# RMSNorm and QKV projection on one core: a longer hand-laid order, and row tiles moved between TensorE and the DMA crossbar

## The chip, the cores and the metric

One core of a Trainium2 chip runs the kernel. Its engines work side by side, each through its own queue of instructions in order: TensorE (PE in the profile, PEld for its weight loads) multiplies matrices and writes PSUM; VectorE (DVE), ScalarE (ACT) and GpSimd (POOL) do elementwise work; SyncE (SP) issues the DMAs, which sixteen DMA engines carry out. The metric is the device time of one execution in microseconds (us), the median of several runs.

## The reference

```python
def reference(x, gamma, w_qkv, eps):
    rms = np.sqrt(np.mean(x ** 2, axis=-1, keepdims=True) + eps)
    x_norm = x / rms * gamma
    return np.matmul(x_norm, w_qkv).astype(np.float32)
```

`x` is 8 x 1024 rows of 768 numbers, `w_qkv` is 768 x 2304, all float32; `gamma` has 768 entries. So 8192 rows are normalised and multiplied into 8192 x 2304 outputs.

## The kernel before

**Tiles.** The 8192 rows are 64 row tiles of 128. A matrix product on TensorE contracts over partitions, so each row tile has to be transposed: its 768 columns become six blocks of 128 x 128 (`xT`). The weights come in 16 pieces (`load_w`), are multiplied by gamma and turned to bf16 (`conv`) into `w_b`.

**Two methods.** Row tiles 0 to 3 are multiplied plainly (`mm`, six blocks per 512 columns), and their results scaled and copied out (`evac`, `store`). All other tiles go in pairs, pair p being tiles 2p and 2p+1, by Strassen-Winograd's seven products in place of eight. For this the 2304 columns are three chunks c of 768, and both operands are cut into quarters: tile 2p gives a11 and a12, tile 2p+1 gives a21 and a22; the weights of a chunk give b11 to b22 and four differences (`quad`, `tsum`), in f16. The sums of the tiles' quarters s1 to s4 come from `osum`, on POOL or DVE.

**One pair.** `load_x` brings a tile (9 buffers), `pstat`, `prms` and `precip` find its scale, `pcast` writes the scaled tile in f16 (`xb`, 4 buffers). It is transposed in one of two ways: `ptr` has TensorE transpose it into PSUM, six matmuls against an identity, and `pcp` copies it to `xT` on DVE or ACT; or `pxbar` (L585) has the DMA crossbar do it, one DMA issued by SP from `xb` to `xT` (10 buffers). Tiles 4 to 15 take the first way, 16 to 63 the second. `product(p, c, i)` is the i-th of seven products, three matmuls of 384 columns (L619). Products 1, 6, 7 and 4 add up in one PSUM bank "a", 2 has bank "b", 5 and 3 have bank "c". Between the additions the partial sums are copied out by `hold` (L626 on DVE, L628 on ACT, 6 buffers); `join` (L637, DVE) adds a bank to a held part and writes a piece of the output tile, `last` (L641, ACT) writes the fourth piece. `pstore` (L647) stores half an output tile, or the whole of a chunk's 768 columns. The output tiles have 12 buffers of 1024 columns. PSUM has eight banks, all in one pool (`psum`, bufs=8).

**What sets the order.** Nothing is moved by the program itself: every operation is given a time, all are sorted by it, and in this order each goes to its engine's queue. Up to `HEAD_END` the times stand in a list written out beforehand, `PLAN`; the pairs from `STEADY` on come from a loop with a fixed rhythm of 7 slots of 0.4875 us per chunk, that starts at `HEAD_END`:

```python
    for p in range(STEADY, MT // 2):
        for c in range(N_CH):
            z = HEAD_END + 7 * SLOT * ((p - STEADY) * N_CH + c)
```

A pair's loads, casts and crossbar transposes are due 28 to 103 slots ahead of its products, so those of the loop's first pairs fall among the list's entries. The times only sort: on the chip an instruction starts when its queue reaches it and its inputs and its buffer are there. SP's queue too is in order; a store or transpose that waits for its data keeps all later DMAs waiting.

The entries at equal places in the list are (time, operation, arguments): `product` has pair, chunk, product; `hold` pair, chunk, bank, name, engine; `join` pair, chunk, the output's quarter, bank, held part; `pstore` pair, chunk, tile of the pair, half.

Of the kernel before, what the change touches and what calls it, by code (L numbers as in the profile page):

```python
# [15 lines left out]
HEAD_END = 138.94  # L16
STEADY = 12

PLAN = [
    (0.000, "load_x", 2), (4.040, "stat", 2), (4.041, "cast", 2, "DVE"), (4.042, "load_x", 1), (4.043, "load_x", 0),  # L20
    (4.044, "load_w", 0), (4.045, "load_w", 1), (5.240, "stat", 1), (5.241, "cast", 1, "DVE"), (5.530, "recip", 2),
    (5.531, "gamma_in"), (6.820, "cast", 0, "ACT"), (6.821, "tr", 2), (6.822, "tr", 1), (6.823, "cp", 1, "DVE"),
    (6.824, "load_w", 3), (8.141, "conv", 0, 0, "ACT"), (8.142, "cp", 2, "DVE"), (8.143, "conv", 0, 1, "DVE"),
    (9.461, "conv", 3, 4, "POOL"), (9.462, "stat", 0), (9.463, "idle", 6, 512), (9.464, "load_w", 2),
    (9.465, "tr", 0), (9.466, "conv", 1, 2, "DVE"), (9.467, "cp", 0, "DVE"), (9.468, "load_x", 3),
    (9.469, "load_w", 4), (9.731, "bound", 0, 0, "DVE"), (11.772, "conv", 4, 5, "DVE"), (11.773, "load_w", 7),
    (11.774, "load_w", 5), (11.775, "mm", 1, 0, "01"), (11.776, "cast", 3, "ACT"), (11.777, "mm", 1, 0, "2"),
    (11.778, "mm", 2, 0, "012"), (11.779, "mm", 0, 0, "2"), (11.780, "mm", 0, 0, "4"), (11.781, "mm", 1, 0, "4"),
    (11.782, "conv", 2, 3, "POOL"), (11.783, "mm", 2, 0, "4"), (13.092, "conv", 7, 5, "POOL"),
    (13.093, "mm", 2, 0, "3"), (13.094, "mm", 0, 0, "3"), (13.095, "mm", 1, 0, "3"), (13.096, "bound", 0, 1, "DVE"),  # L30
    (13.097, "stat", 3), (14.022, "recip", 3), (14.023, "mm", 0, 0, "01"), (14.122, "recip", 0), (14.123, "tr", 3),
    (14.124, "mm", 0, 0, "5"), (14.125, "load_w", 6), (14.222, "recip", 1), (14.223, "conv", 7, 4, "ACT"),
    (14.322, "cp", 3, "DVE"), (14.822, "evac", 0, 0, "DVE"), (14.823, "mm", 2, 0, "5"), (14.824, "mm", 1, 0, "5"),
    (14.825, "mm", 1, 512, "45"), (14.826, "load_w", 9), (14.827, "conv", 5, 0, "POOL"), (14.828, "mm", 2, 512, "45"),
    (14.829, "mm", 0, 512, "54"), (14.830, "conv", 5, 1, "ACT"), (15.227, "mm", 3, 512, "45"),
    (15.659, "mm", 3, 512, "01"), (15.660, "load_w", 8), (16.091, "mm", 1, 512, "01"), (16.092, "evac", 2, 0, "ACT"),
    (16.093, "load_w", 10), (16.094, "conv", 6, 2, "ACT"), (16.523, "mm", 2, 512, "01"),
    (16.524, "conv", 6, 3, "POOL"), (16.954, "mm", 0, 512, "01"), (17.386, "mm", 1, 512, "23"),
    (17.818, "mm", 0, 512, "23"), (17.819, "evac", 1, 0, "DVE"), (18.249, "mm", 2, 512, "23"),
    (18.250, "bound", 0, 2, "DVE"), (18.251, "conv", 9, 3, "POOL"), (18.394, "fold", 0), (18.684, "bound_tr", 0),  # L40
    (18.685, "load_x", 5), (18.686, "load_x", 4), (18.687, "conv", 8, 0, "DVE"), (18.688, "conv", 9, 2, "POOL"),
    (18.804, "mm", 3, 512, "23"), (18.805, "bound", 1, 0, "ACT"), (19.004, "bound_top", 0),
    (19.695, "conv", 10, 4, "POOL"), (19.696, "mm", 1, 1024, "23"), (20.375, "conv", 10, 5, "POOL"),
    (20.376, "load_w", 13), (20.377, "bound_all", 0), (20.378, "evac", 0, 512, "DVE"), (20.379, "conv", 8, 1, "ACT"),
    (20.380, "mm", 3, 1024, "01"), (20.381, "bound", 1, 1, "ACT"), (20.382, "scales", 0),
    (20.383, "mm", 0, 1024, "23"), (20.384, "evac", 2, 512, "DVE"), (20.967, "quad", 0, "b11", "DVE"),
    (20.968, "load_x", 7), (20.969, "pstat", 5), (20.970, "load_w", 12), (25.307, "conv", 12, 2, "POOL"),
    (25.308, "pstat", 4), (26.165, "conv", 12, 3, "POOL"), (26.166, "bound", 1, 2, "ACT"),
    (26.167, "mm", 0, 1024, "01"), (26.168, "quad", 0, "b12", "DVE"), (26.169, "quad", 0, "b22", "DVE"),
    (26.170, "mm", 3, 1024, "23"), (26.171, "mm", 3, 1024, "45"), (26.172, "tsum", 0, "t1", "DVE"),  # L50
    (26.173, "tsum", 0, "t3", "DVE"), (26.174, "prms", 2), (26.175, "conv", 13, 4, "ACT"),
    (26.176, "mm", 1, 1024, "45"), (26.845, "conv", 13, 5, "POOL"), (26.846, "load_w", 15), (26.847, "precip", 2),
    (27.525, "conv", 15, 3, "POOL"), (27.526, "mm", 0, 1024, "45"), (27.527, "mm", 1, 1024, "01"),
    (27.528, "evac", 0, 1024, "ACT"), (27.529, "load_x", 6), (27.530, "mm", 2, 1024, "45"),
    (27.531, "mm", 3, 0, "012345"), (27.532, "fold", 1), (27.533, "bound_tr", 1), (27.534, "pcast", 5),
    (27.535, "mm", 2, 1024, "01"), (27.536, "bound_top", 1), (27.537, "mm", 2, 1024, "23"),
    (27.538, "evac", 3, 1024, "ACT"), (27.539, "ptr", 5), (27.540, "evac", 1, 1024, "DVE"), (27.541, "bound_all", 1),
    (27.542, "evac", 3, 512, "ACT"), (27.543, "load_w", 14), (27.544, "evac", 1, 512, "DVE"),
    (27.545, "mm", 1, 1536, "23"), (27.546, "pcp", 5, "DVE"), (27.547, "mm", 3, 1536, "23"),
    (27.868, "mm", 2, 1536, "45"), (27.869, "load_w", 11), (27.870, "load_x", 13), (27.871, "pstat", 7),  # L60
    (28.300, "mm", 0, 1536, "23"), (28.301, "scales", 1), (28.732, "mm", 0, 1536, "45"),
    (29.163, "mm", 2, 1536, "23"), (29.164, "pstat", 6), (29.165, "evac", 2, 1024, "ACT"), (29.525, "prms", 3),
    (29.526, "pcast", 4), (29.527, "bound", 2, 1, "DVE"), (29.775, "conv", 14, 1, "ACT"), (29.776, "load_x", 9),
    (29.777, "ptr", 4), (30.185, "pcp", 4, "DVE"), (30.186, "conv", 15, 4, "POOL"), (30.187, "conv", 15, 5, "POOL"),
    (30.685, "precip", 3), (30.686, "mm", 1, 2048, "345"), (30.785, "conv", 14, 0, "DVE"),
    (31.575, "tsum", 0, "t2", "DVE"), (31.576, "quad", 1, "b12", "POOL"), (32.275, "quad", 0, "b21", "DVE"),
    (32.276, "conv", 14, 2, "ACT"), (32.277, "mm", 2, 2048, "345"), (32.278, "mm", 1, 1536, "45"),
    (32.279, "load_x", 10), (32.280, "conv", 11, 1, "ACT"), (32.281, "load_x", 8), (32.282, "conv", 11, 0, "POOL"),
    (33.015, "pcast", 6), (33.016, "evac", 3, 0, "ACT"), (33.565, "osum", 2, "s1", "DVE"),
    (34.025, "osum", 2, "s2", "POOL"), (35.405, "quad", 1, "b22", "POOL"), (35.406, "mm", 3, 1536, "45"),  # L70
    (35.407, "bound", 2, 2, "ACT"), (35.408, "mm", 3, 2048, "345"), (35.409, "pcast", 7),
    (35.410, "mm", 3, 1536, "01"), (35.411, "mm", 2, 2048, "012"), (36.675, "quad", 1, "b21", "POOL"),
    (36.676, "mm", 1, 2048, "012"), (36.677, "evac", 1, 2048, "DVE"), (36.678, "mm", 3, 2048, "012"),
    (36.679, "evac", 2, 2048, "DVE"), (36.680, "mm", 2, 1536, "01"), (36.681, "bound", 2, 0, "ACT"),
    (36.682, "load_x", 11), (36.683, "mm", 1, 1536, "01"), (36.684, "fold", 2), (36.685, "evac", 2, 1536, "DVE"),
    (36.686, "mm", 0, 1536, "01"), (36.687, "product", 2, 0, 1), (36.688, "hold", 2, 0, "a", "p1", "ACT"),
    (36.689, "evac", 3, 2048, "ACT"), (36.690, "quad", 1, "b11", "ACT"), (36.691, "product", 2, 0, 2),
    (36.692, "ptr", 6), (36.693, "product", 2, 0, 6), (36.694, "bound_tr", 2), (36.695, "product", 2, 0, 5),
    (36.696, "join", 2, 0, 0, 0, "b", "p1"), (36.697, "bound_top", 2), (36.873, "pcp", 6, "DVE"), (36.940, "ptr", 7),
    (37.500, "pcp", 7, "DVE"), (37.501, "evac", 1, 1536, "ACT"), (37.888, "evac", 0, 1536, "ACT"),  # L80
    (37.889, "mm", 0, 2048, "012"), (37.890, "mm", 0, 2048, "345"), (38.000, "tsum", 1, "t1", "DVE"),
    (38.001, "product", 2, 1, 1), (38.488, "evac", 0, 2048, "ACT"), (38.878, "hold", 2, 0, "c", "p5", "ACT"),
    (38.879, "osum", 3, "s1", "DVE"), (38.880, "store", 3, 0, 0, 1024), (39.020, "osum", 2, "s4", "DVE"),
    (39.340, "osum", 2, "s3", "DVE"), (39.341, "bound_all", 2), (39.378, "evac", 3, 1536, "ACT"),
    (39.978, "hold", 2, 0, "a", "u2", "ACT"), (39.979, "product", 3, 0, 1), (39.980, "tsum", 1, "t2", "DVE"),
# [216 lines left out]
def kernel(  # L302
# [357 lines left out]
    for p in range(STEADY, MT // 2):  # L660
        for c in range(N_CH):
# [5 lines left out]
            if c == 0:  # L667
                odd = p % 2
# [71 lines left out]
```

## Time and profile before

| | |
|---|---|
| median of 3 runs | 362.32 us (362.31 to 363.31) |
| the profiled execution | 362.69 us, of which the span from first to last instruction is 360.7 |
| TensorE busy | 342.9 us, 95% of the span |
| DVE, ACT, POOL busy | 267.0, 244.5 and 124.0 us |
| granted TensorE clock | 0.998 of full speed |
| moved by DMA | 117.61 MB, 326 GB/s in the mean |
| SP's issues | 64 loads of x (384 KB, 6.6 us to landing in the median), 178 stores of 384 KB (5.2), 48 crossbar transposes (5.7) |

A row of a group or of the timeline reads: start or line, engine, operation, `out<-in` by the program's names, shape, count; in the timeline the bracket at the end is the idle time of the engine just before, and what ended it. A row of the waits reads: who waited, for whom, total us, times, longest. In rows of stretches the "DMA share" is the time that packets took over sixteen engines' time; packets of one engine overlap, so it can go over 1.

### The profile page before, as it was taken

To read this page: it belongs to the slowest core of one execution; us is meant where nothing else is said; L and a number is where in the kernel's file an instruction comes from. 1 tells how busy PE (TensorE), PEld (TensorE's weight loads), DVE (VectorE), ACT (ScalarE), POOL (GpSimd) and SP (SyncE) were. 2 spreads that over 40 slices of the span, in tenths; PEclk is the share of its full clock that TensorE was granted. 3 is DMA by queue.
4 is the path that set the end of the run, shared out by engine and by line. 5 is a ranking of instruction groups with operands and counts; after the bars stand their busy time and mean duration, and the time that the engine had idled before them with its cause. 6 is when DMAs were issued, how large, how long until landed. Compare 5 with 4: busy or idle time off the path is not lost.

```text
span 360.7 us, 6633 instructions
## 1 busy us (share of the span) xinstructions
PE 342.9 (95%) x2116; PEld 203.3 (56%) x2119; DVE 267.0 (74%) x498; ACT 244.5 (68%) x500; POOL 124.0 (34%) x141
## 2 busy tenths in 40 slices
PE   4899999999959989999999999999999999999995
PEld 2445566666536545655566666666666666666662
DVE  3898999878567955777879586776778676775763
ACT  5798889866727756767576775857666766855553
POOL 0337365331060433142334160708061523434000
PEclk9999999999999999999999999999999999999999
DMA  7999559698999999999999999999999999996565
GB/s 252 393 387 391 211 197 391 226 303 264 281 328 305 308 309 393 327 361 341 391 342 412 310 391 342 387 341 392 346 365 395 332 393 297 382 276 275 223 261 219
DMA packets 79693, 117.61 MB, mean 326 GB/s; under 512 B 42790, under 2 KB 44588, under 8 KB 79660
## 3 DMA queue, kind: packets, MB, share of 16 engines
q1 hardware_dynamic: 79648, 117.20, 97.0%
q8 instruction: 16, 0.26, 0.3%
q14 instruction: 17, 0.14, 0.1%
q10 hardware_dynamic: 12, 0.00, 0.0%
HBM read 32.25 MB, written 75.50 MB: 299 GB/s over the span
## 4 chain that ended last, share of the span: by engine, by line
PE 81%; DMA 13%; DVE 2%; SPq 1%; issue 1%; ACT 0%; POOL 0%; DVEq 0%
PE pm L619 79%; DMA out_dram<-ot 5%; DMA x_t<-in_x_dram 5%; DMA wq<-in_w_qkv_dram 3%; DVE ot L637 1%; PE pm L604 1%; PE pm L449 1%; SPq L375 1%; SPq L370 1%; DVE su L599 0%; DVE wq L557 0%; POOL w_b L385 0%; DVE xb L581 0%; DVE pp L626 0%; ACT pp L628 0%
## 5 line engine op out<-in xcount | busy, mean ns | idle before, releaser
L619 PE MATMUL pm<-wq,su 128*128 128x384 f16 x1080 | 204.6, 326 | 3.6 <-POOL su L599 3.6
L637 DVE SCALAR_TENSOR_TENSOR ot<-pm,sc,pp 128x384 f32<-128x384 f32 x270 | 155.8, 612 | 57.3 <-PE pm L619 40.6
L628 ACT ACTIVATE pp<-pm,sc 128x384 f32<-128x384 f32 x208 | 116.5, 580 | 79.4 <-PE pm L619 76.0
L619 PE MATMUL pm<-wq,xT 128*128 128x384 f16 x810 | 160.9, 326 | 3.7 <-DVE ot L637 3.7
L619 PEld LDWEIGHTS <-su 128*128 128x128 f16 x1080 | 105.2, 98 | 73.2 <-POOL su L599 4.0
L619 PEld LDWEIGHTS <-xT 128*128 128x128 f16 x810 | 79.0, 98 | 57.3 <-issue 6.0
L599 POOL TENSOR_TENSOR su<-xT 128x384 f16<-128x384 f16 x53 | 48.6, 936 | 164.6 <-DMA xT<-xb 104.8
L641 ACT ACTIVATE ot<-pm,sc 128x384 f32<-128x384 f32 x90 | 51.6, 575 | 25.0 <-PE pm L619 24.6
L626 DVE TENSOR_SCALAR pp<-pm,sc 128x384 f32<-128x384 f32 x62 | 38.0, 614 | 22.4 <-PE pm L619 22.2
L567 ACT ACTIVATE sq<-x_t 128x768 bf16<-128x768 f32 x60 | 50.2, 837 | 1.3 <-DMA x_t<-in_x_dram 1.1
L581 DVE TENSOR_SCALAR xb<-x_t,rstd 128x768 f16<-128x768 f32 x60 | 41.8, 700 | 0.5
L599 POOL TENSOR_TENSOR su<-su,xT 128x384 f16<-128x384 f16 x29 | 27.7, 956 | 9.6 <-DVE su L599 9.4
L599 POOL TENSOR_TENSOR su<-xT,su 128x384 f16<-128x384 f16 x29 | 27.6, 952 | 8.3 <-DVE su L599 6.1
L449 PE MATMUL pm<-w_b,xT 128*128 128x512 bf16 (+1 forms) x117 | 24.9, 357 | 1.9 <-ACT w_b L383 1.2
L449 PEld LDWEIGHTS <-xT 128*128 128x128 bf16 x120 | 11.3, 98 | 12.4 <-issue 2.4
L385 POOL TENSOR_SCALAR w_b<-wq,g_sb 128x512 bf16<-128x512 f32 (+1 forms) x16 | 10.7, 682 | 19.6 <-DMA wq<-in_w_qkv_dram 19.3
L567 ACT ACTIVATION_READ_ACCUMULATOR sq<-x_t 128x1 f32 x60 | 11.6, 193 | 0.0
L571 ACT ACTIVATE rms<-ssq,eps_sb 128x2 f32<-128x2 f32 x30 | 8.8, 294 | 0.2
L557 DVE TENSOR_TENSOR wq<-wq 128x1152 f16<-128x1152 f16 x11 | 8.9, 815 | 0.0
L551 POOL TENSOR_SCALAR wq<-w_b,inv 128x1152 f16<-128x1152 bf16 x6 | 7.3, 1222 | 3.7 <-DVE inv L535 3.7
L509 ACT ACTIVATE sq<-w_b 128x1536 bf16<-128x1536 bf16 x5 | 7.4, 1481 | 0.4
L506 DVE TENSOR_REDUCE bnd<-w_b 128x1 f32<-128x1536 bf16 x4 | 7.0, 1748 | 0.7 <-POOL w_b L385 0.6
(51 smaller groups left out, 82.6 us busy)
## 6 DMA issues: line engine op xcount, KB each, us to landing
out_dram<-ot SPq DMA_DIRECT2D x178, 384.0 KB, 5.2
x_t<-in_x_dram SPq DMA_DIRECT2D x64, 384.0 KB, 6.6
wq<-in_w_qkv_dram SPq DMA_DIRECT2D x10, 512.0 KB, 8.5
out_dram<-ot SPq DMA_DIRECT2D x8, 512.0 KB, 5.7
wq<-in_w_qkv_dram SPq DMA_DIRECT2D x4, 256.0 KB, 7.1
wq<-in_w_qkv_dram SPq DMA_DIRECT2D x2, 384.0 KB, 10.3
xT<-xb SPq DMA_TRANSPOSE x48, 5.7
out_dram<-ot SPq DMA_DIRECT2D x4, 192.0 KB, 2.2
```

The source lines that it names most:

```text
L385: nc.gpsimd.tensor_scalar(out=o, in0=i, scalar1=g, scalar2=1.0, op0=mult, op1=mult)
L449: nc.tensor.matmul(out=PM[t, n0][:, :nl], lhsT=XT[t][:, ko, :], rhs=w_b[:, ko, n0:n0 + nl], start=(b == 1), stop=(b == KO))
L557: (nc.vector if eng == "DVE" else nc.gpsimd).tensor_tensor(out=new_quad(c, q), in0=i0, in1=i1, op=sub)
L567: nc.scalar.activation(out=sq, in_=X[t], func=AF.Square, accum_out=SS[p][:, t % 2:t % 2 + 1])
L571: nc.scalar.activation(out=r, in_=SS[p], func=AF.Sqrt, scale=inv_k, bias=eps_sb)
L581: nc.vector.tensor_scalar(out=XB[t], in0=X[t], scalar1=SS[t // 2][:, t % 2:t % 2 + 1], scalar2=None, op0=mult)
L599: (nc.vector if eng == "DVE" else nc.gpsimd).tensor_tensor(out=block(p, q), in0=block(p, x), in1=block(p, y), op=op)
L619: nc.tensor.matmul(out=PB[k][:, :CW], lhsT=block(p, a)[:, ko, :], rhs=WQ[c, b][:, ko, :], start=(first and ko == 0), stop=(ko == KO // 2 - ...
L626: nc.vector.tensor_scalar(out=o, in0=pb, scalar1=SC[c], scalar2=None, op0=mult)
L628: nc.scalar.activation(out=o, in_=pb, func=AF.Copy, scale=SC[c], bias=0.0)
L637: nc.vector.scalar_tensor_tensor(out=result(p, c, i, j), in0=PB[p, c, bank][:, :CW], scalar=SC[c], in1=PART[p, c, held], op0=mult, op1=add)
L641: nc.scalar.activation(out=result(p, c, 1, 0), in_=PB[p, c, "a"][:, :CW], func=AF.Copy, scale=SC[c], bias=0.0)
```

## The change

`STEADY` goes from 12 to 15: three more pairs (12, 13 and 14) are laid out in the list instead of the loop, and `HEAD_END` goes from 138.94 to 165.20. The whole list is new, the first weights and plain products included, with other times and another order on every engine's queue; the operations are those of before, except for the transposes. Eleven row tiles are transposed by TensorE: 4 to 9, 11, 13, 15, 17 and 19, so from pair 5 to pair 9 one tile of two. The others, 10, 12, 14, 16, 18 and 20 to 63, take the crossbar; the first such transpose stands at 60.903 in the list, where it stood at 83.371. In the loop the parity that picks a pair's lead is turned, so that pair 15 has the lead that pair 12 had.

The diff, cut to its core (`...` for what is left out; the removed list is shown by its transposes, the new one by its first entries, its transposes on the crossbar and its end):

```diff
--- before.py
+++ after.py
-HEAD_END = 138.94
-STEADY = 12
+HEAD_END = 165.20
+STEADY = 15
 
 PLAN = [
...
-    (27.538, "evac", 3, 1024, "ACT"), (27.539, "ptr", 5), (27.540, "evac", 1, 1024, "DVE"), (27.541, "bound_all", 1),
...
-    (29.777, "ptr", 4), (30.185, "pcp", 4, "DVE"), (30.186, "conv", 15, 4, "POOL"), (30.187, "conv", 15, 5, "POOL"),
...
-    (36.696, "join", 2, 0, 0, 0, "b", "p1"), (36.697, "bound_top", 2), (36.873, "pcp", 6, "DVE"), (36.940, "ptr", 7),
...
-    (51.450, "last", 3, 1), (51.725, "ptr", 8), (51.950, "hold", 3, 2, "a", "p1", "ACT"), (52.085, "ptr", 9),
...
-    (55.282, "hold", 3, 2, "a", "u2", "ACT"), (55.283, "hold", 2, 2, "c", "p5", "ACT"), (55.284, "ptr", 10),
...
-    (57.290, "pcp", 10, "ACT"), (57.680, "ptr", 11), (57.681, "pstore", 2, 1, 1), (58.040, "product", 4, 0, 5),
...
-    (63.617, "product", 4, 1, 3), (63.618, "pcast", 13), (63.890, "ptr", 12), (64.255, "join", 4, 1, 0, 1, "c", "u2"),
...
-    (64.808, "store", 1, 1, 1024, 1024), (64.809, "pstore", 2, 2, 1), (64.810, "ptr", 13),
...
-    (70.179, "ptr", 14), (70.533, "pcp", 14, "ACT"), (70.534, "product", 5, 2, 6), (70.820, "product", 5, 0, 5),
...
-    (71.511, "ptr", 15), (72.148, "join", 5, 0, 1, 1, "a", "p5"), (72.149, "product", 5, 0, 2),
...
-    (83.371, "pxbar", 16), (83.855, "product", 6, 0, 7), (84.543, "join", 6, 0, 1, 1, "a", "p5"),
...
-    (90.595, "hold", 7, 1, "c", "p5", "ACT"), (90.596, "pxbar", 18), (90.597, "product", 6, 2, 7),
...
-    (94.093, "product", 7, 0, 2), (94.580, "product", 6, 2, 4), (94.581, "pxbar", 17),
-    (94.582, "osum", 8, "s1", "POOL"), (94.583, "pstore", 5, 2, 0), (94.584, "pxbar", 19), (94.585, "pstat", 20),
...
+    (0.000, "load_x", 2), (4.040, "stat", 2), (4.041, "cast", 2, "DVE"), (4.042, "load_x", 1), (5.240, "stat", 1),
+    (5.241, "load_x", 3), (5.242, "cast", 1, "DVE"), (5.243, "load_x", 0), (5.530, "recip", 2), (5.531, "load_w", 4),
+    (5.532, "load_w", 1), (5.533, "load_w", 0), (5.534, "gamma_in"), (5.535, "idle", 6, 512), (5.536, "tr", 2),
+    (8.470, "conv", 4, 5, "POOL"), (8.471, "cp", 2, "DVE"), (8.472, "cast", 3, "DVE"), (9.150, "conv", 1, 2, "POOL"),
+    (9.151, "tr", 1), (9.152, "tr", 3), (9.153, "recip", 1), (9.154, "cast", 0, "DVE"), (9.155, "cp", 1, "ACT"),
...
+    (60.902, "product", 4, 0, 7), (60.903, "pxbar", 10), (61.102, "hold", 4, 1, "c", "p5", "ACT"),
...
+    (66.338, "hold", 5, 2, "c", "p5", "ACT"), (66.349, "pstat", 15), (66.350, "pxbar", 12),
...
+    (72.474, "product", 5, 0, 3), (72.475, "pcast", 14), (72.476, "pxbar", 14), (72.962, "product", 6, 0, 5),
...
+    (74.564, "pcast", 17), (74.565, "ptr", 15), (74.566, "product", 5, 2, 7), (74.567, "product", 6, 0, 1),
...
+    (77.141, "hold", 6, 1, "a", "p1", "ACT"), (77.142, "load_x", 22), (77.143, "ptr", 17),
...
+    (87.005, "load_x", 23), (87.006, "ptr", 19), (87.007, "pxbar", 16), (87.008, "product", 6, 1, 3),
...
+    (90.819, "pxbar", 18), (90.820, "product", 7, 0, 3), (91.367, "join", 7, 0, 0, 1, "c", "u2"),
...
+    (103.293, "pstat", 24), (103.294, "pcast", 20), (103.295, "join", 8, 0, 1, 1, "a", "p5"), (103.296, "pxbar", 21),
...
+    (109.567, "hold", 9, 1, "c", "p5", "DVE"), (109.568, "pxbar", 22), (110.117, "join", 8, 2, 1, 1, "a", "p5"),
...
+    (110.669, "hold", 9, 0, "a", "u2", "ACT"), (110.670, "product", 9, 0, 5), (110.671, "pxbar", 20),
...
+    (113.529, "product", 9, 0, 4), (113.530, "pxbar", 23), (113.837, "join", 9, 2, 0, 0, "b", "p1"),
...
+    (116.655, "pxbar", 27), (116.656, "product", 10, 0, 1), (116.657, "pxbar", 25),
...
+    (131.281, "last", 10, 0), (131.282, "product", 10, 2, 3), (131.567, "product", 4, 2, 1), (131.568, "pxbar", 24),
+    (131.569, "pxbar", 26), (132.054, "product", 11, 2, 1), (132.542, "product", 10, 2, 4),
...
+    (136.929, "product", 11, 2, 5), (136.930, "last", 11, 1), (136.931, "pxbar", 28), (136.932, "pcast", 29),
...
+    (141.317, "product", 12, 0, 1), (141.804, "product", 11, 2, 2), (141.805, "pxbar", 29), (141.806, "last", 11, 2),
...
+    (163.257, "hold", 13, 1, "a", "u2", "DVE"), (163.742, "product", 13, 1, 7), (164.229, "product", 14, 2, 2),
+    (164.230, "hold", 14, 2, "c", "p5", "ACT"), (164.231, "hold", 13, 1, "c", "p5", "DVE"),
+    (164.632, "join", 13, 1, 1, 1, "a", "p5"), (164.717, "product", 14, 1, 7), (165.204, "product", 14, 2, 6),
+    (165.404, "join", 14, 1, 1, 1, "a", "p5"), (165.692, "product", 14, 2, 3),
+    (165.892, "hold", 14, 2, "a", "u2", "ACT"), (165.954, "join", 14, 2, 0, 0, "b", "p1"),
+    (166.179, "product", 13, 2, 6), (166.867, "hold", 13, 2, "a", "u2", "ACT"), (166.868, "product", 13, 1, 4),
+    (167.367, "last", 13, 1), (167.368, "product", 14, 1, 4), (167.369, "join", 14, 2, 0, 1, "c", "u2"),
+    (167.867, "last", 14, 1), (167.868, "pstore", 14, 2, 0), (168.007, "pstore", 13, 1, 1),
+    (168.507, "pstore", 14, 1, 1), (168.508, "product", 14, 2, 7), (168.509, "join", 14, 2, 1, 1, "a", "p5"),
+    (168.510, "product", 13, 2, 5), (168.617, "product", 13, 2, 7), (169.104, "product", 14, 2, 4),
+    (169.592, "product", 13, 1, 2), (169.593, "hold", 13, 2, "c", "p5", "DVE"),
+    (169.594, "join", 13, 2, 1, 1, "a", "p5"), (170.079, "product", 13, 2, 3), (170.080, "last", 14, 2),
+    (170.767, "join", 13, 2, 0, 1, "c", "u2"), (170.768, "pstore", 14, 2, 1), (170.769, "product", 13, 2, 4),
+    (171.054, "product", 13, 1, 3), (171.254, "last", 13, 2), (171.742, "join", 13, 1, 0, 1, "c", "u2"),
+    (171.743, "pstore", 13, 2, 0), (172.292, "join", 13, 1, 0, 0, "b", "p1"), (172.293, "pstore", 13, 2, 1),
+    (172.982, "pstore", 13, 1, 0),
...
@@ -665,7 +732,7 @@
                 at(z + u * SLOT, fn, *args)
 
             if c == 0:
-                odd = p % 2
+                odd = (p + 1) % 2
                 for i in range(2):
```

## The prediction

> **What bounds the kernel now.** I read the page first, then stretches of time, then the chain.
>
> ```profile
> span 360.7 us, 6633 instructions
> PE 342.9 (95%) x2116; PEld 203.3 (56%) x2119; DVE 267.0 (74%) x498; ACT 244.5 (68%) x500; POOL 124.0 (34%) x141
> ```
>
> TensorE (PE) is the bound, but the 95% is a mean over unlike stages. The next rows are stretches of time; after each engine's busy time and count come the granted clock, the DMA share and GB/s.
>
> ```profile
> 44.00:97.00 53.00, 52.93 (x358) 32.95 (x358) 45.63 (x91) 41.23 (x84) 18.61 (x17) 1.00 0.81 276
> 97.00:178.00 81.00, 74.36 (x450) 43.65 (x449) 58.22 (x107) 50.21 (x109) 28.47 (x31) 1.00 1.06 336
> 178.00:356.00 178.00, 177.93 (x1095) 107.04 (x1094) 127.95 (x233) 117.24 (x245) 58.66 (x64) 1.00 1.01 336
> 40.00:60.00 20.00, 19.61 (x136) 12.07 (x136) 19.08 (x39) 17.55 (x36) 10.13 (x9) 1.00 0.63 235
> 60.00:80.00 20.00, 20.00 (x143) 12.62 (x141) 16.41 (x32) 16.01 (x35) 7.51 (x8) 1.00 0.80 288
> 100.00:120.00 20.00, 16.98 (x103) 10.07 (x104) 14.40 (x28) 11.83 (x26) 8.18 (x10) 1.00 1.03 333
> ```
>
> From 178 on, 1095 matmuls fill 178 us: 162.6 ns each, nothing lost. Between 97 and 178 there are 450, worth 73.2 us; so 81 - 73.2 = **7.8 us are lost there**. I count matmuls because the busy sum (6.6 us missing) hides part of each stall in the modelled ends. Before 97 nothing is lost after the start-up. The DMA share tells why: 0.63 and 0.80 while PE ran well, 1.03 where it did not. The chain and the timeline name the waits:
>
> ```profile
> 98.43 6.01 DMA out_dram<-ot
> 123.65 9.76 DMA out_dram<-ot x2
> 134.08 3.58 DMA out_dram<-ot
> ```
>
> ```profile
> 99.76 0.62 DVE L637 SCALAR_TENSOR_TENSOR ot<-pm,sc,pp 128x384 f32<-128x384 f32 x1 [3.81 <-DMA out_dram<-ot]
> 101.19 0.91 POOL L599 TENSOR_TENSOR su<-xT 128x384 f16<-128x384 f16 x1 [18.20 <-DMA xT<-xb]
> 102.16 0.66 PE L619 MATMUL pm<-wq,su 128*128 128x384 f16 x3 [3.57 <-POOL su L599]
> ```
>
> A join waits for a store to free an output tile; POOL's sum waits for a crossbar tile; PE waits for the sum. Both are DMAs that land late. The crossbar's row and the price of one wait of PE for a bank:
>
> ```profile
> DMA to landing us min/median/max: 2.7/5.7/8.6
> PE pm L619 <- DVE ot L637: 3.7, 8, 1.2
> ```
>
> **How I read the list.** Its times only sort, but distances in it can be read on the chip while nothing stalls: pair 8's first product has 95.07 and starts at 96.96 (1.9 later, as pairs 4 to 7 do), pair 15's would have 169.65 and starts at 181.25. The 7.8 us of stalls are most of that slip.
>
> **1. HEAD_END itself is worth almost nothing.** Three pairs of 10.24 us bring the old 138.94 to 169.65; the new list puts pair 15 at 165.20, 4.45 us earlier. But it leaves 13 products of older pairs behind that point, the old one 5; in the rhythm of the loop 2 always stand there. Extra work: 11 x 0.488 = 5.4 us against 3 x 0.488 = 1.5. So 170.6 against 171.1: the same PE work but for the next item. The gain can only be stalls removed.
>
> **2. Transposes.** Twelve PE tiles become eleven: six transposes less. The chain has the row `53.98 0.67 PE pm L604 x12`, so one tile is 0.33 us: **-0.3**. The Trainium skill ("TensorE: Matmul & The Clock Gate", Part 4: PE-mode transpose) gives about 275 ns for one transpose inside a kernel; six would make -1.65. The row decides: in this stream they run at 56 ns. One copy of 0.55 us (DVE) or 0.81 us (ACT) goes; both engines have idle time (DVE 74%, ACT 68%), so nothing. On the crossbar go tiles 10, 12, 14 (new), off it 17 and 19: one more, 1.47 us of SP's issue time by its median and one tile of DMA time. Order moves far more than number.
>
> **3. DMA, the term that pays.** Packet records give 66.6 us of all sixteen engines for the 48 crossbar tiles (768 packets of 256 B each): 1.39 us a tile; a load of x or a 384 KB store is 128 packets of 3072 B, 1.0 us. Summing what each list gives SP: up to list time 90, 74 us before and 91 after; from 90 to 140, **61 us before and 50 us after**. The rows above show 1.03 to 1.06 engine-shares taken where it is full, so 61 in 50 can't be served and 50 in 50 can. The early transposes, loads, and stores no longer held (the old list holds one of pair 6 for 57 us after its data) go into the stretch that had 0.63 and 0.80. A page speaks against this: "DMA: Bandwidth & Descriptors" (Latency and other measured facts) gives 261 GB/s for transposes with a non-contiguous middle dimension, so 0.75 us for 196,608 B. By it the old stretch, with twelve tiles, would need 53 us in 50 and hardly be over-full, and I would take half of the gain below, 3.9. The measured 1.39 decides.
> The second measure is the distance from a crossbar issue (its place in SP's order, and not before its cast) to its first reader. Before: 3.7 us for tile 17, 5.7 for 19, 5.0 for 23, against a landing of 8.0 us for tile 17: hence the wait at 102. After: 5.1 for tile 10, 6.2 for 14, 7.1 for 20, all others 9 or more. Output tiles: before, an allocation came 1.7 to 3.1 us after the store that frees its tile (twelve tiles, counted along the list) five times between 95 and 104; after, none under 7.6 us from 57 to 165. So I take the **7.8 as removed**, and for what comes back 5.7 - 5.1 = 0.6 at tile 10 plus 0.4 for the rest: **+1.0** (bounds 0 and, at 8.6 each, 3.5 + 2.4 + 1.5 = 7.4; the median because 40 to 60 had the emptiest queue).
> SP waits in order: each transpose waits there for its cast and holds the stores behind it, 5.9 us at worst before; the three early ones meet a queue of two or three stores, hidden by free output tiles.
>
> **4. The seam at 165: a new wait.** Eleven extra products of pairs 13 and 14 are interleaved with pair 15, and more groups want a PSUM bank than the eight there are. At product (15,0,5) open are (13,1)a,c, (13,2)a, (14,1)a, (14,2)a,b,c and (15,0)a. By hand, with 0.49 for a product, 0.16 until it can be read, 0.61 for a join or hold on DVE, 0.70 for a cast, from the end of product (14,1,7): DVE does join (14,1) 0.16 to 0.77, cast 35 to 1.47, join (14,2,0,0) to 2.08, which frees the bank; PE wanted it at 0.98: **1.1**. Then (14,2,3) ends at 3.1; (15,0,2) needs the bank that join (14,2,0,1) frees, behind a hold: 3.97, **0.9**. Likewise (13,1,2) waits for a `last` on ACT, 0.6, and (13,1,6) for a hold on ACT, 0.5. Together **+3.1**. No row shows this seam; the nearest is the bank waits above, 8 with 3.7 us and 1.2 at most, which are of the same size each. Bounds 0 (DVE ahead of its order) and 5 (a ninth bank assigned less luckily). Queued behind the waiting product are all later ones; ACT and DVE wait with PE, POOL and SP don't.
>
> **5. The head.** Four loads of x go ahead of the first weights instead of three, though that piece is now 256 KB instead of 512: +0.3; ahead of the last piece (landed at 31.98) stand seven loads instead of eight: -1.0. I take **0**, bounds -1.0 and +1.5. Parity changes with STEADY (15 is treated as 12 was), so the loop's rhythm is unchanged: 0.
>
> **Sum.** 360.7 - 7.8 - 0.3 + 1.0 + 3.1 + 0 = 356.7. The profiled execution took 362.69, so 2.0 lie around its span; the median is 362.32. I take the difference, -4.0, from the median: **358.3 us**. A change within 0.3% (361.2 to 363.4) can't be told from none.
>
> **Rivals.**
> *A, all of it:* seam and leftovers cost 0.5 in all; 362.3 - 8.1 + 0.5 = 354.7. For it: the wide distances. Against it: the bank count.
> *B, the crowd moves:* the list has 52 us of DMA from 140 to 180 against 40 in the next forty. If stores land late there, half of the 7.8 returns: 362.2 (360.5 to 363.3). Against it: PE is then 5 to 8 us behind the list, which gives the DMA that time.
> *C, slower:* PE waits for crossbar tiles. If landing takes L, tiles 10, 14 and 20 wait L - 5.1, L - 6.2 and L - 7.1. The 4.0 gained with 1.0 for leftovers are gone at 5.0 of such waits: L = 7.8. At L = 10: 4.9 + 3.8 + 2.9 and 1.4 for four others, 13.0; 360.7 - 8.1 + 3.1 + 13.0 gives 368.7, or 370.3 against the median. For it: three tiles before took 6.4 to 8.0. Against it: the median 5.7, and that was in the full queue.
>
> **Chances.** The likeliest 0.47 (own range 356 to 360.5), A 0.15, B 0.20, C 0.18. Faster: 0.47 + 0.15 and half of B, 0.72; same: 0.08 of B; slower: C and the rest of B, 0.20. The range takes in A and nearly all of B: 354.3 to 363.5.
>
> **What would show it.** Right: no join waiting for a store between 97 and 165, 40 to 80 with a DMA share clearly above 0.8, pair 15 mixed with PE waits for DVE of about 1 us twice between 165 and 175, and a full PE afterwards. Wrong: POOL sums waiting for crossbar tiles with PE behind them between 60 and 120 (C), joins waiting for stores after 140 (B), or more than 1.5 us lost before 44.

## The result, and the profile after

The changed kernel takes **356.12 us** in the median of four runs (355.91 to 356.93); the kernel before took 362.31 beside it (361.89 to 363.31). The ratio is 0.983, with a 95% interval of 0.980 to 0.986: 6.2 us, or 1.7%, faster. The prediction had 358.3 us with a range of 354.3 to 363.5: right in sign and inside its range, and 2.2 us too slow. The profiled execution took 356.93 us with a span of 354.8.

The first lines of the page of the changed kernel: span, then busy time and share of each engine.

```profile
span 354.8 us, 6638 instructions
PE 343.6 (97%) x2113; PEld 203.6 (57%) x2113; DVE 267.8 (75%) x504; ACT 243.7 (69%) x498; POOL 116.9 (33%) x135
```

TensorE's busy time is the same, 343.6 against 342.9; the span is 5.9 us shorter. The same stretches of time as before the change (busy time and count of PE, PEld, DVE, ACT and POOL, then granted clock, DMA share, GB/s):

```profile
40.00:60.00 20.00, 20.00 (x136) 12.16 (x134) 19.69 (x40) 18.45 (x38) 9.79 (x9) 1.00 1.03 397
60.00:80.00 20.00, 20.00 (x137) 12.45 (x135) 16.72 (x34) 16.56 (x36) 5.40 (x6) 1.00 1.05 359
100.00:120.00 20.00, 20.00 (x125) 12.03 (x123) 15.93 (x32) 11.79 (x24) 3.60 (x5) 1.00 0.94 287
...
44.00:97.00 53.00, 53.00 (x355) 32.74 (x355) 46.08 (x91) 45.56 (x97) 16.62 (x17) 1.00 1.07 368
97.00:178.00 81.00, 78.95 (x483) 47.03 (x482) 65.00 (x122) 49.95 (x105) 24.93 (x28) 1.00 1.04 333
178.00:350.00 172.00, 171.82 (x1057) 103.27 (x1056) 123.25 (x226) 111.51 (x233) 54.36 (x61) 1.00 0.97 321
```

From 97 to 178, 483 matmuls run where there were 450. From 40 to 80 the DMA share is 1.03 and 1.05, where it had 0.63 and 0.80; from 100 to 120 it is 0.94 and PE is full. The kernel before has this row in its list of waits:

```profile
DVE ot L637 <- DMA out_dram<-ot: 10.4, 7, 3.8
```

In the changed kernel no VectorE (DVE) join waits for a store between 44 and 180 us; one wait of 0.4 us is left, at 232 us. The crossbar's landing row:

```profile
DMA to landing us min/median/max: 2.5/5.0/7.4
```

A landing is only a little shorter than before (2.7/5.7/8.6). What the changed kernel still loses lies at the seam; its timeline, with only the rows that free a bank or wait for one:

```profile
168.51 0.61 DVE L648 TENSOR_SCALAR xb<-x_t,rstd 128x768 f16<-128x768 f32 x1
...
169.70 1.14 PE L686 MATMUL pm<-wq,su 128*128 128x384 f16 x6 [0.79 <-DVE ot L704]
171.62 0.65 PE L686 MATMUL pm<-wq,xT 128*128 128x384 f16 x3 [0.78 <-DVE ot L704]
178.29 0.65 PE L686 MATMUL pm<-wq,xT 128*128 128x384 f16 x3 [0.18 <-ACT ot L708]
```

The first PE row is product (15,0,5), which waits for a join that stands behind a cast; the second is (15,0,2), the third (13,1,2). Lines of the changed file are those of before plus 67, so L619 is now L686, L637 is L704, L581 is L648.

**The lag of TensorE.** The brackets show idle time with modelled ends, so a stall is measured in another way. For each product, take its start on the chip and subtract all TensorE work queued ahead of it (0.4875 us a product, 0.335 us a tile transposed by TensorE, the plain products likewise). The lag grows only where PE stalls or works more slowly, so it gives each stall its size:

| us of lag gained | before | after |
|---|---|---|
| at 48 us, the whole head | 10.51 | 10.17 |
| 97 to 178 us, other products: some nine stalls, most behind stores and crossbar tiles | 8.24 (the first 3.73) | 0 |
| product (12,1,4) at 153 us | 0 | 0.65 |
| seam: (13,1,6), (15,0,5), (15,0,2), (13,1,2) | 0 | 0.15 + 0.95 + 0.94 + 0.34 = 2.38 |
| last product | 0.38 | 0.38 |

With one transposed tile less (0.33): 360.7 - 8.24 - 0.33 + 0.65 + 2.38 - 0.34 = 354.8, the span.

### The profile page after: what moved, and what is told of

It is laid out like the page before. It is cut to its first block, busy times and chain, and to the rows that moved or that the text cites. A ratio compares the mean times of both kernels' runs of the same rounds, so it can differ in the third digit from the quotient of the medians.

```text
span 354.8 us, 6638 instructions
## 1 busy us (share of the span) xinstructions
PE 343.6 (97%) x2113; PEld 203.6 (57%) x2113; DVE 267.8 (75%) x504; ACT 243.7 (69%) x498; POOL 116.9 (33%) x135
## 4 chain that ended last, share of the span: by engine, by line
PE 54%; DVE 1%; ACT 0%; issue 0%
PE pm L686 54%; DVE ot L704 1%; DVE xb L648 0%; ACT ot L708 0%; DVE pp L693 0%
## 5 line engine op out<-in xcount | busy, mean ns | idle before, releaser
L686 PE MATMUL pm<-wq,su 128*128 128x384 f16 x1080 | 204.9, 326 | 0.8 <-DVE ot L704 0.8
L704 DVE SCALAR_TENSOR_TENSOR ot<-pm,sc,pp 128x384 f32<-128x384 f32 x270 | 156.6, 613 | 47.6 <-PE pm L686 42.3
L695 ACT ACTIVATE pp<-pm,sc 128x384 f32<-128x384 f32 x203 | 114.0, 582 | 75.3 <-PE pm L686 71.9
L686 PE MATMUL pm<-wq,xT 128*128 128x384 f16 x810 | 160.9, 326 | 1.7 <-DVE ot L704 1.5
L686 PEld LDWEIGHTS <-su 128*128 128x128 f16 x1080 | 105.2, 98 | 70.1 <-issue 1.2
L686 PEld LDWEIGHTS <-xT 128*128 128x128 f16 x810 | 79.1, 98 | 54.7 <-issue 2.6
L666 POOL TENSOR_TENSOR su<-xT 128x384 f16<-128x384 f16 x51 | 46.3, 925 | 154.3 <-PE pm L686 84.9
L693 DVE TENSOR_SCALAR pp<-pm,sc 128x384 f32<-128x384 f32 x67 | 40.9, 616 | 23.5 <-PE pm L686 23.0
L648 DVE TENSOR_SCALAR xb<-x_t,rstd 128x768 f16<-128x768 f32 x60 | 40.3, 678 | 0.4
L666 POOL TENSOR_TENSOR su<-su,xT 128x384 f16<-128x384 f16 x27 | 25.3, 938 | 26.5 <-DVE su L666 14.6
L666 POOL TENSOR_TENSOR su<-xT,su 128x384 f16<-128x384 f16 x27 | 25.2, 935 | 10.0 <-DVE su L666 6.7
L452 POOL TENSOR_SCALAR w_b<-wq,g_sb 128x512 bf16<-128x512 f32 (+1 forms) x14 | 9.1, 662 | 14.0 <-DMA wq<-in_w_qkv_dram 14.0
L618 POOL TENSOR_SCALAR wq<-w_b,inv 128x1152 f16<-128x1152 bf16 x9 | 11.2, 1261 | 4.9 <-DVE inv L602 4.9
L573 DVE TENSOR_REDUCE bnd<-w_b 128x1 f32<-128x1536 bf16 x5 | 8.7, 1747 | 0.3 <-ACT w_b L450 0.3
L534 ACT ACTIVATE ot<-pm,rstd 128x512 f32<-128x512 f32 x10 | 6.6, 684 | 1.1 <-PE pm L516 1.0
```

What stands on the lines that cost most here:

```text
L452: nc.gpsimd.tensor_scalar(out=o, in0=i, scalar1=g, scalar2=1.0, op0=mult, op1=mult)
L618: nc.gpsimd.tensor_scalar(out=o, in0=quad_view(c, q), scalar1=INV[c], scalar2=1.0, op0=mult, op1=mult)
L648: nc.vector.tensor_scalar(out=XB[t], in0=X[t], scalar1=SS[t // 2][:, t % 2:t % 2 + 1], scalar2=None, op0=mult)
L666: (nc.vector if eng == "DVE" else nc.gpsimd).tensor_tensor(out=block(p, q), in0=block(p, x), in1=block(p, y), op=op)
L686: nc.tensor.matmul(out=PB[k][:, :CW], lhsT=block(p, a)[:, ko, :], rhs=WQ[c, b][:, ko, :], start=(first and ko == 0), stop=(ko == KO // 2 - ...
L693: nc.vector.tensor_scalar(out=o, in0=pb, scalar1=SC[c], scalar2=None, op0=mult)
```

## The experiments

**Theory T.** The gain is that stores, loads and crossbar transposes are issued early enough to land before they are needed. The number of TensorE transposes and HEAD_END matter little, and the seam gives 2.4 us back. **Rivals:** R1, taking every other crossbar transpose out of the crowded time makes the gain; R2, it comes from the new order of products, casts and copies on the engines, or the new head; R3, early crossbar transposes make it.

Every group of runs has its own runs of the kernel before (medians 362.23, 362.63, 362.72), so ratios are compared. "Lost" is lag gained between 48 and 200 us in the profiled execution, half clock included (last section).

| kernel | us | ratio, 95% interval | lost |
|---|---|---|---|
| before | 362.31 | 1 | 8.2 |
| after | 356.12 | 0.983 (0.980 to 0.986) | 3.0 |
| x1: before, half stores | 357.45 | 0.988 (0.983 to 0.993) | 4.4 |
| x6: before, 47 DMAs early | 360.22 | 0.994 (0.991 to 0.997) | 4.4 |
| x8: before, crossbar of tile 17 early | 363.65 | 1.004 (1.002 to 1.006) | 10.1 |
| x7: before, both of these | 356.04 | 0.983 (0.980 to 0.986) | 0.5 |
| x2: after, half stores | 355.75 | 0.981 (0.978 to 0.985) | 2.4 |
| x9: after, 32 stores late | 368.94 | 1.017 (1.014 to 1.021) | 17.8 |
| x4: after, 17 and 19 on the crossbar | 354.95 | 0.979 (0.977 to 0.982) | 2.9 |
| x5: after, 10, 12, 14 by TensorE | 356.49 | 0.985 (0.982 to 0.988) | 2.9 |
| x3: after, HEAD_END 167.20 | 354.91 | 0.980 (0.976 to 0.983) | 1.8 |
| after again | 355.56 | 0.981 (0.978 to 0.984) | 2.8 |
| c2: x3 and x4 | 354.27 | 0.978 (0.976 to 0.981) | 1.6 |
| c3: c2, 13 and 15 on the crossbar too | 359.16 | 0.991 (0.989 to 0.994) | 7.8 |

### x1: is it the amount stored?

```diff
     def pstore(p, c, i, *half):
-        j0, j1 = (half[0], half[0] + 1) if half else (0, 2)
+        j0, j1 = (half[0], half[0] + 1) if half else (0, 1)
```

> The kernel before, whose paired stores of 768 columns write only their left 384; the right 384 columns of those rows stay unwritten, everything else is as in the kernel before. Theory T (the change gains because the DMA work before the seam is spread, so that stores and crossbar transposes land in time): with much less to store, the 7.8 us that TensorE loses between 97 and 178 us in the kernel before mostly go, and the run takes 354 to 356 us; the waits of VectorE for output buffers whose stores have not landed (10.4 us in 7 waits in the kernel before) fall to under 2 us. Rival R2 (the gain comes from the new order of products, casts and copies on the engines, not from the DMA queue): the order is the old one, so the run stays at 361 to 362.5 us.

Measured: 357.45 us. Both were wrong: R2 clearly, and T in its size. In the profiled execution 4.4 of the 8.2 us of stalls stay; it was the slowest of the four (361.26 us, the others 356.81 to 357.65), and its head alone was 2.6 us later than before. DVE still waits 6.7 us for stores, where T had under 2. The chain of x1 (start, length, what) and its stretch 97 to 178:

```profile
98.32 0.73 SPq L585
...
99.10 0.58 SPq L370
...
99.72 4.48 DMA out_dram<-ot
...
104.23 0.63 DVE ot L637
```

```profile
97.00:178.00 81.00, 77.43 (x474) 46.04 (x472) 58.77 (x111) 53.61 (x115) 29.84 (x33) 1.00 0.93 252
```

Only 252 GB/s are moved instead of 336, and still a join waits for a store: the store stands in SP's queue behind a crossbar transpose and a load, is issued at 99.7 us and lands 4.5 us later, after DVE has waited 1.7 us for it. **Less to move helps; a store that stands late in the queue stays late.**

### x6, x8 and x7: only SP's order

x6 gives some of the kernel before's stores and loads an earlier place; x8 does so for one crossbar transpose, x7 for both. Nothing else is touched.

```diff
+    EARLY = {("store", 2, 0, 0, 1024): 21.0, ("load_x", 17): 30.2, ("load_x", 15): 33.7, ("load_x", 12): 36.1,
+             ...
+             ("pstore", 5, 0, 1): 77.4, ("pstore", 5, 2, 1): 79.3, ("pstore", 5, 0, 0): 79.6,
+             ...
     for time, op, *args in PLAN:
-        at(time, ops[op], *args)
+        at(EARLY.get((op, *args), time), ops[op], *args)
```

```diff
-    (94.093, "product", 7, 0, 2), (94.580, "product", 6, 2, 4), (94.581, "pxbar", 17),
+    (94.093, "product", 7, 0, 2), (94.580, "product", 6, 2, 4), (90.5955, "pxbar", 17),
```

The expectations speak of 55 entries; eight of them are loads that the loop issues and the edit did not reach. 47 DMAs moved (37 stores, 10 loads), by 4 to 108 us of list time, 17 in the median.

> The kernel before, with 55 of its stores and row-tile loads between 21 and 136 us moved forward in SP's order to the list time at which what they move is there; the order of PE, DVE, ACT and POOL, the twelve TensorE transposes and the crossbar transposes are untouched. By the list, 83 us of 16-engine DMA time then stand before 90 (before 74, changed kernel 91) and 57 between 90 and 140 (61 and 50). Theory T: part of the 7.8 us of stalls between 97 and 178 us goes, those that wait for a store, but the crossbar transpose of tile 17 still stands less than 4 us ahead of its first sum: 357.5 to 361 us. Rival R2 (the engines' order makes the gain): 361.5 to 363 us.

Measured: 360.22 us, in T's range. No join waits for a store any more; the crossbar transpose of tile 17 is now the wait, as T said (the timeline, PE's row with its wait):

```profile
99.78 1.11 POOL L599 TENSOR_TENSOR su<-xT 128x384 f16<-128x384 f16 x1 [16.48 <-DMA xT<-xb]
...
100.95 0.66 PE L619 MATMUL pm<-wq,su 128*128 128x384 f16 x3 [2.06 <-POOL su L599]
```

> The kernel before with one crossbar transpose, that of tile 17, moved forward in SP's order by 4.0 us of list time (94.581 to 90.596, ahead of that of tile 18); its cast, the sums, the products and all stores and loads stay. Theory T: the 3.7 us stall at product (8,0,5) is a crossbar landing that ends last, so it goes, but VectorE still waits for output buffers whose stores are late, some 2 us of it take the stall's place: 358.5 to 360.5 us. Rival (the stall is only the first of a queue of late DMA work, and its loss is found again at the next wait): 361.5 to 362.5 us.

Measured: 363.65 us, slower than before, and outside both expectations. The first stall does go. The kernel before issues two loads and a store just ahead of tile 17's transpose (timeline, SP):

```profile
91.41 1.06 SPq L370 DMA_DIRECT2D x_t<-in_x_dram  x2
92.51 0.43 SPq L647 DMA_DIRECT2D out_dram<-ot  x1
93.11 2.26 SPq L585 DMA_TRANSPOSE xT<-xb  x1
```

By the records of each DMA, these loads landed at 97.72 and 98.68 us and the transpose at 101.06, 8.0 us after its issue. In x8 it was issued ahead of them at 91.79 and landed at 94.52, after 2.7 us. In both, every DMA issued from 87 to 100 us whose landing is recorded landed in the order of issue. But the joins behind it then wait for the late stores instead (timeline of x8):

```profile
100.75 0.62 DVE L637 SCALAR_TENSOR_TENSOR ot<-pm,sc,pp 128x384 f32<-128x384 f32 x1 [4.68 <-DMA out_dram<-ot]
...
105.33 0.62 DVE L637 SCALAR_TENSOR_TENSOR ot<-pm,sc,pp 128x384 f32<-128x384 f32 x1 [2.46 <-DMA out_dram<-ot]
105.99 1.12 PE L619 MATMUL pm<-wq,xT 128*128 128x384 f16 x3 [3.93 <-DVE ot L637]
```

At 105.99 PE loses 4.1 us of lag. The same store ends the stalls in both kernels: it landed at 104.45 in the kernel before, where PE went on at 105.14, and at 105.30 here. So the wait for tile 17 had hidden this one, and taking it away gained nothing. Then 2.3 us more are lost at half clock (last section), which the kernel before was spared; without them x8 would have lost 7.8, not 10.1.

> The same move of tile 17's crossbar transpose on top of the earlier run that moved 55 stores and row-tile loads of the kernel before forward in SP's order (that run: 360.2 us). Engines' orders and the twelve TensorE transposes are those of the kernel before. Theory T: with late stores and the late crossbar transpose both gone, the stretch from 97 to 178 us loses at most 1 us, and the run stands where the changed kernel does, 355 to 357.5 us. Rival R2 (a part of the gain comes from the engines' new order, the head laid out anew or the eleven transposes): 358.5 to 360 us.

Measured: **356.04 us, ratio 0.983, the changed kernel's own.** Stretch and chain of x7:

```profile
97.00:178.00 81.00, 80.82 (x498) 48.44 (x496) 61.33 (x114) 55.95 (x120) 30.78 (x34) 1.00 1.09 343
```

```profile
79.98 45.01 PE pm L619 x277
...
125.01 24.06 PE pm L619 x147
```

498 matmuls instead of 450, and a chain that is TensorE alone. So with the old order on all engines, the old head and the twelve TensorE transposes, moving 48 DMAs in SP's queue is enough for the whole gain. R2 and R3 fall. It takes both parts: alone they give -2.0 and +1.0 us, together -6.6. The changed kernel loses 2.5 us more than x7 after 48 us and starts 0.9 us sooner (below); in their medians both come to the same time.

### x2 and x9: the same two knobs on the changed kernel

x2 is x1's edit in the changed kernel.

> The changed kernel with the same cut: its paired stores of 768 columns write only their left 384, the right 384 stay unwritten. Theory T: nothing in the changed kernel waits for DMA any more; what it still loses (0.9 us at product (12,1,4), 2.4 us at the seam) are waits of TensorE for casts, joins and PSUM banks. So 355.6 to 356.2 us, at most 0.5 us below the changed kernel's 356.1. Rival (DMA crowding is still worth something after the change, in late crossbar landings): 1 to 3 us less, 353 to 355 us.

Measured: 355.75 us, as T said; the seam's stalls stand in it as in the changed kernel, 0.16, 0.95, 0.94 and 0.34 us. With less to store nothing is gained beyond the noise, so the amount of DMA is no longer a limit. x9 makes its stores late:

```diff
     for time, op, *args in PLAN:
-        at(time, ops[op], *args)
+        at(time + 10.0 if op == "pstore" and 55 < time < 105 else time, ops[op], *args)
```

> The changed kernel with the 32 paired stores that stand between 55 and 105 us of the list held back by 10 us in SP's order, all else as it is: the kernel before's lateness of stores put into the changed kernel (13 us of list time between a store's data and its place in place of 4). Theory T: VectorE waits for output buffers again and TensorE behind it, 2 to 6 us: 358 to 362 us, stalls between 65 and 125 us. Rival R2 (where the stores stand in the queue doesn't matter with the new order on the engines): 355.5 to 357 us.

Measured: 368.94 us. T has the sign, and is too low by 7. Timeline of x9, joins and PE:

```profile
80.05 0.62 DVE L704 SCALAR_TENSOR_TENSOR ot<-pm,sc,pp 128x384 f32<-128x384 f32 x1 [2.46 <-DMA out_dram<-ot]
...
91.14 0.62 DVE L704 SCALAR_TENSOR_TENSOR ot<-pm,sc,pp 128x384 f32<-128x384 f32 x1 [2.90 <-DMA out_dram<-ot]
...
149.21 0.36 DVE L666 TENSOR_TENSOR su<-xT 128x384 f16<-128x384 f16 x1 [6.31 <-DMA xT<-xb]
...
150.15 1.12 PE L686 MATMUL pm<-wq,xT 128*128 128x384 f16 x3 [5.46 <-DVE ot L704]
```

Four stalls behind waits for stores, up to 92 us, cost PE 6.3 us (0.56, 1.68, 2.08, 1.96 of lag), just above T's 2 to 6. Then crossbar tiles are late at 124 and 149 us, which T had not counted. A sum on DVE waits 6.3 us for a tile, the join behind it waits, and PE with it: 1.0 and 5.6 of lag, and 1.4 more at half clock. The moved stores now stand among these transposes in the one queue of SP; that this makes them late fits the in-order landings above, but no run took it apart.

### x4, x5: who transposes

```diff
-    (77.143, "ptr", 17), ... (78.417, "pcp", 17, "ACT"), ... (87.006, "ptr", 19), ... (88.892, "pcp", 19, "ACT"),
+    (77.143, "pxbar", 17), ... (87.006, "pxbar", 19),
```

> The changed kernel with tiles 17 and 19 transposed by the crossbar again, at the places of SP's order where their TensorE transposes stood in the list, 15 and 13 us ahead of their first sums; nine TensorE transposes remain. Theory T (what counts is that a crossbar transpose is issued early enough, not who does it): 0.7 us less work for TensorE against 2.8 us more DMA time in a full stretch, so within 1 us of the changed kernel, 355.2 to 357.2 us. Rival R1 (the gain comes from taking every other crossbar transpose out of the crowded time): 358 us or more, with PE waiting for sums at 92 to 105 us.

Measured: 354.95 us, 0.6 to 1.2 us less than the two medians of the changed kernel; 0.67 is the TensorE work. PE doesn't stall at 92 to 105 us. R1 falls: the crossbar can do tiles 17 and 19 if asked 13 to 15 us ahead.

```diff
-    (60.903, "pxbar", 10), ... (66.350, "pxbar", 12), ... (72.476, "pxbar", 14),
+    (59.928, "ptr", 10), (60.569, "pcp", 10, "ACT"), ... (66.350, "ptr", 12), (67.318, "pcp", 12, "ACT"),
+    ... (73.220, "ptr", 14), (73.640, "pcp", 14, "ACT"),
```

> The changed kernel with tiles 10, 12 and 14, which it moved to the crossbar, transposed by TensorE again; fourteen TensorE transposes. Theory T: three times 0.33 us more of TensorE and 4.2 us less of DMA time in a stretch that nothing waits for: 356.6 to 357.8 us, about 1 us slower than the changed kernel. Rival R3 (crossbar transposes early are where the change gains): 358.5 us or more, or with DMA relief worth something there: 355 us or less.

Measured: 356.49 us, 0.4 to 0.9 us more than the changed kernel. This is just under T's range; its three times 0.33 fits within the noise. R3 falls here too.

### x3, c2, c3: can the seam be had back?

```diff
-HEAD_END = 165.20
+HEAD_END = 167.20
```

> The changed kernel with HEAD_END 167.20 in place of 165.20: all of the loop's work stands 2.0 us (four products) later in the merge with the list, nothing else is changed. Theory T: the seam's three stalls (1.10 at product (15,0,5), 0.94 at (15,0,2), 0.34 at (13,1,2)) come from the interleaving of the loop's first groups with 13 products left over from the list; worked by hand with the engines' durations of the trace, this shift leaves 0.5 us of 2.4, so 353.7 to 354.6 us. Rival: the stalls only move, or the later casts and loads of pairs 15 to 17 cost as much again: 355.7 to 357 us.

Measured: 354.91 us, between the two expectations. The seam's stalls are gone, and another has come, at product (15,0,4), worth 1.24 us. Timeline of x3:

```profile
179.47 0.83 DVE L648 TENSOR_SCALAR xb<-x_t,rstd 128x768 f16<-128x768 f32 x1
180.22 1.13 DVE L704 SCALAR_TENSOR_TENSOR ot<-pm,sc,pp 128x384 f32<-128x384 f32 x2
180.87 0.65 PE L686 MATMUL pm<-wq,xT 128*128 128x384 f16 x3 [1.08 <-DVE ot L704]
```

A cast of 0.83 us, 0.2 longer than most (last section), stands ahead of the joins that free PE's banks. Half of the seam comes back.

> The changed kernel as it is, for comparison within one group of runs: 355.9 to 356.9 us, as in its own runs. No theory says otherwise; its trace also tells whether the 0.9 us at product (12,1,4) belongs to the kernel or to one execution (in two of the runs on it the stall was gone, in one it was 0.4 us).

Measured: 355.56 us. The stall at (12,1,4) is 0.37 here, so it is partly one execution's; the seam's are 0.16, 0.95, 0.94 and 0.34, as in the first trace.

c2 joins the edits of x3 and x4:

> The changed kernel with both edits that had gained: HEAD_END 167.20 in place of 165.20, and tiles 17 and 19 transposed by the crossbar (nine TensorE transposes). If the gains of 1.2 us each are independent: 353.7 us (353.2 to 354.3). Rival (both take away the same delay, or the later loop meets later crossbar landings): 354.6 to 355.5 us.

Measured: 354.27 us (353.26 to 355.59), 1.3 below the changed kernel in the same group. It has the shortest time and span (351.1) of all kernels here, and lies at the edge of the range for independent gains. Its interval (0.976 to 0.981) overlaps the changed kernel's (0.978 to 0.984), so whether the two gains add can't be told.

c3 puts tiles 13 and 15 on the crossbar as well:

```diff
-    (63.339, "ptr", 13), ... (64.389, "pcp", 13, "ACT"), ... (74.565, "ptr", 15), ... (74.785, "pcp", 15, "ACT"),
+    (63.339, "pxbar", 13), ... (72.474, "pxbar", 15),
```

> The same with tiles 13 and 15 on the crossbar as well, that of tile 13 in the place of its TensorE transposes (6.4 us of list time ahead of its first sum), that of tile 15 at 72.474, 6.8 us ahead of its first sum; seven TensorE transposes. Theory T: another 0.7 us of TensorE work off, 353.0 us (352.4 to 354.0), if both land in time. Rival (two more crossbar transposes of 1.4 us of all 16 engines in the full stretch make landings of 7 us, and a sum waits): 354.5 to 357 us, with POOL or VectorE waiting for xT at 69.7 or 79.2 us.

Measured: 359.16 us, the rival's case and worse. Timeline of c3, SP's issue and PE:

```profile
87.17 4.28 SPq L652 DMA_TRANSPOSE xT<-xb  x2
```

```profile
95.54 1.15 PE L686 MATMUL pm<-wq,xT 128*128 128x384 f16 x6 [2.86 <-DMA xT<-xb]
```

PE first loses 1.0 us at 75 and 77 us, where pair 6 waits for tile 12 and a DVE sum. The big stall (3.0 of lag, and 1.6 after it at half clock) is one that no expectation had named: product (8,1,1) wants tile 16, whose transpose stands in SP's queue right behind that of tile 19. In c2 tile 16 was issued at 87.0 us and landed at 91.5, 0.3 us ahead of its product. In c3 it was issued at 89.2 and landed at 95.5: 2.2 us later to be issued, and 1.9 us longer on the way. The DMAs issued in the five microseconds ahead of it took 5.9 to 7.7 us to land, again in order. That the two added transposes (2.8 us of DMA time by the prediction's 1.39) made this backlog fits; no run took it apart.

## Why the prediction was right, step by step

**Step 1 (HEAD_END is worth nothing in itself): holds.** x7 has the old HEAD_END and the time of the changed kernel, and moving it by 2.0 us (x3) changed the seam's stalls and little else.

**Step 2 (transposes, -0.3): holds.** x4 (two fewer, -0.6 to -1.2) and x5 (three more, +0.4 to +0.9) lie around 0.33 a tile. The Trainium skill's price that was weighed there ("TensorE: Matmul & The Clock Gate", Part 4: PE-mode transpose), about 275 ns a transpose, would have made 3.3 and 5.0 us of them.

**Step 3 (DMA, -7.8 and +1.0): right result, reasons wrong in part.** The stalls from 97 to 178 us were 8.24 us by lag and all went; counting matmuls had 7.8. But the first measure, "61 in 50 can't be served and 50 in 50 can", fails. x1's list asks for some 45 from 90 to 140 and loses 4.4 us, x7's asks for 57 and loses 0.5. The sum over a stretch doesn't decide. The second measure, the distance from a DMA's place to its reader, points the right way (x7 and x9 change it and get the gain and a loss), but it was set against a landing time taken as given. For tile 17 the issue came only 0.9 us earlier in x7 (92.23 against 93.11); what went from 8.0 to at most 2.7 (its sum starts at 94.94) is the landing, because of what is issued just ahead of it. The +1.0 for landings that come back was near what was lost by luck alone: tile 10 landed 4.7 us after its issue and held back nothing in this trace (0.1 us in the second one). What came was 0.65 us at (12,1,4), a bank that a join frees behind a slow cast.

**Step 4 (seam, +3.1): mechanism right, size off.** The two waits for DVE, forecast as 1.1 and 0.9, were 0.95 and 0.94. The two for ACT, (13,1,2) and (13,1,6), were 0.34 and 0.15 instead of 0.6 and 0.5; (13,1,6) stands at 0.15 to 0.16 in every trace of the new list with HEAD_END at 165.20. Sum 2.38.

**Step 5 (head, 0): off by 0.34** in the compared executions. Over all nine profiled executions with the new list the lag at 48 us is 8.8 to 10.9, in the median 9.65; over the five with the old, 10.5 to 13.2, in the median 10.8. So the new head is worth about -1.2, just past the bound of -1.0. That it pays for part of the seam's excess over x7 is an inference from these sums; no run changed the head alone.

**The sum.** From the predicted change of -4.0 to the measured -5.9 of span: 0.44 from step 3's size, 0.35 from its leftovers, 0.72 from step 4, 0.34 from step 5, and 0.03 from step 2. All five lean the same way: the forecast was too slow by a sum of small cautions, not by one wrong step.

**The rivals.** A (354.7) was near, but for a wrong reason: seam and leftovers cost 3.0, not 0.5. B did not happen. C did not happen here, and c3 shows how close it was: two more crossbar transposes and PE waits for tiles. C's three tiles (10, 14 and 20) were not the ones; 12 and 16 were, 16 landing late behind a backed-up queue.

## What to carry to other kernels

For DMAs in one in-order queue, don't ask how many microseconds of transfer a stretch holds, but for each one when its reader needs it and what stands in front of it in the queue: tile 17's transpose landed 8.0 us after its issue behind two loads and a store, and 2.7 us after it ahead of them. Removing one late DMA can gain nothing when another late one is waiting behind it (x8), so take the late ones together. Before laying out a long list anew, try to move only the DMAs in the old one: x7 had the whole gain from 48 moved entries.

## What the runs showed of the hardware

**A stall can cost more than its length.** After a long wait, TensorE sometimes went on at half its clock. The stretches of x6 and x8 behind their stalls (the third number from the end is the granted clock):

```profile
102.00:105.00 3.00, 3.00 (x11) 1.46 (x10) 0.62 (x1) 0.23 (x1) 2.67 (x4) 0.50 0.84 337
```

```profile
105.90:111.00 5.10, 5.01 (x17) 2.35 (x17) 3.02 (x7) 2.12 (x4) 0.46 (x1) 0.51 0.71 280
```

Each product then costs about 0.96 us instead of 0.49; in x8 that added 2.3 us to a wait of 3.9. It followed waits of 2.06 (x6), 2.86 (c3), 3.93 (x8) and 5.46 us (x9), but not the 3.57 us in the kernel before. The Trainium skill ("TensorE: Matmul & The Clock Gate", HAM oscillation) warns of idle gaps over some 3.4 us; here shorter ones were enough, and one longer was not. The traces' records of the clock narrow it down. In every execution the clock changes only at whole multiples of 3.41 us after its first change. The four half-clock stretches behind these waits each begin where such a window of 3.41 us ends in which PE, by its records, had been idle for 2.06 (x6), 2.18 (c3), 2.77 (x8) and 3.41 us (x9). The 3.57 us of the kernel before fell across an edge, 1.58 in one window and 1.99 in the next, and the clock stayed. So what fits these five is the idle time within one window, with a limit between 1.99 and 2.06 us, and not the length of the wait. The limit isn't a fixed one: in the first 30 us and near the end, windows with 1.8 and 1.9 us idle were followed by half clock, and in x8 a second window with 1.97 idle stayed at it.

**A cast on DVE can be slower beside a sum on POOL.** Timeline of the changed kernel, just ahead of the stall at (12,1,4):

```profile
150.71 1.78 POOL L666 TENSOR_TENSOR su<-xT,su 128x384 f16<-128x384 f16 x2
151.66 1.25 DVE L648 TENSOR_SCALAR xb<-x_t,rstd 128x768 f16<-128x768 f32 x1
...
153.49 0.81 PE L686 MATMUL pm<-wq,xT 128*128 128x384 f16 x4 [0.49 <-DVE ot L704]
```

Of this kernel's 60 casts in f16, the 10 that overlap a POOL sum by more than 0.1 us take 0.61 to 1.30 us, 1.12 in the median; the other 50 take 0.60 to 0.62. In the second trace of the same kernel (after again) the median of such casts is 0.68, so an overlap does not always slow a cast, but every slow cast in both has one. The stall at (12,1,4) follows the cast just ahead of it: with 1.25 us here PE loses 0.65, with 0.97 in the second trace 0.37, and with 0.61 in x2, where no POOL sum runs beside it, nothing. That the overlap is the cause of the slow cast was not tried by itself.
